# Layer 1's gate and up products by seven half-size products, and sums of squares placed behind later tiles

## The chip, the cores and the metric

The kernel runs on one core of one Trainium2 chip. The metric is the device time of one execution in microseconds, as a median of several runs. The engines of the core are TensorE (PE, with its weight loads PEld), VectorE (DVE), ScalarE (ACT), GpSimd (POOL) and SyncE (SP), which issues most of the transfers.

## What is computed

Two layers of a transformer over 512 latent tokens and 256 context tokens, 1024 features wide, all in float32. Each layer is a token mixer followed by a SwiGLU of 2816 features; each is modulated by a conditioning vector. Layer 0 carries latents and context, layer 1 returns the latents only.

```python
def modulate(x, shift, scale):
    return rms_norm(x) * (1 + scale) + shift

def swiglu(h, w_gate_up, w_down):
    g, u = jnp.split(h @ w_gate_up, 2, axis=-1)
    return (jax.nn.silu(g) * u) @ w_down
...
    for l in range(DEPTH):
        ...
        h_lat = h_lat + g_a * o_lat
        h_lat = h_lat + g_f * swiglu(modulate(h_lat, sh_f, sc_f), ffn_w_gate_up[l], ffn_w_down[l])
        if ctx_out:
            h_ctx = h_ctx + cg_a * o_ctx
            h_ctx = h_ctx + cg_f * swiglu(modulate(h_ctx, csh_f, csc_f), ffn_w_gate_up[l], ffn_w_down[l])
    return rms_norm(h_lat, final_norm)
```

## The kernel before

**Layout.** Features lie on the 128 partitions, tokens along the free axis: eight tiles of 128 x 768 hold the stream (512 latent tokens, `LATS`, then 256 of context, `CTXS`). Every product is made from high and low parts: an operand is cast to a rounded high part on ScalarE (L305, L1193, L1325) and the rest is subtracted on VectorE (L306, L1194, L1326), and each 128-deep step takes three matmuls, high x high, high x low, low x high (L315 to L317 in `mm3`; L1188 to L1190 in `product`; L728 to L730 in `three`).

**Layer 0's SwiGLU (`ffn0`)** already works by seven products. The 768 tokens are two halves of 384 (`TOK1`, `TOK2`), the 1024 input features two halves of four tiles, and gate and up are the two rows of the weight matrix. `combined` makes the operands: "11", "12", "21", "22" are the modulated stream by feature half and token half, and `sums` makes T1 to T4 from their differences, each split into high and low parts. The class `Pair` handles one of the 22 tiles of 128 hidden features, gate and up together. `weights` loads both, splits the gate weights and makes four sums of half weights (S1 to S4, lines L1213 to L1221) with their parts. `head` makes the products with "11" and "21", `body` those with T2, T3 and T1, `tail` those with "22" and T4. Around them ScalarE copies or applies Silu (L1231 to L1246), VectorE adds (L1232, L1242, L1248) and multiplies gate by up (L1250). The first hidden tile, `first_pair`, is made by eight plain products, in the order in which the halves' norms are ready. Pairs are worked in chunks (`CHUNKS0`); after each chunk the down products of its hidden tiles are added to the stream, tile by tile (`add_residual`, L1076).

**Layer 1's SwiGLU (`ffn`)** is plain: for each of 22 hidden tiles, gate and then up, eight input tiles by three matmuls on all 512 latent tokens; for the first two hidden tiles the two halves of 256 tokens (`HALVES`) go one after the other, as their norms become ready. Silu is at L1320, the product at L1324. Four chunks (`CHUNKS`). The input comes from `modulated`: one scale (L382), one ScalarE shift to the high part (L383) and one VectorE low part (L384) for each tile and half.

**Norms and `output`.** `output` makes the last products of a block stream by stream (a stream is a set of token columns), adds them to the residual and adds each tile's squares (ScalarE L347, the add L350 on GpSimd or VectorE). A stream's `Norm.rest` then runs in steps during the next stream's tiles, the first after tile 0: column sums by matmul (L360), square root (L361), reciprocal (L362), a diagonal (L363), a broadcast by matmul (L368), a copy to the tile `nb` (L369), and then `use` for each of the eight tiles. Engines work in order; the order on each is fixed by a scheduler from program order and its own timeline.

**Background.** The modulation vectors are products of `mod_w` with the conditioning. `bg()` advances this work by a step; late in the kernel a step loads a row block into the one tile `rope` and sums it on VectorE (L214). In layer 0's SwiGLU two steps follow each pair (`BG[1]`), and what is left is done in layer 1's `bg(j < 8)` or on demand in `mod()`.

**Buffers.** `b` 24, `st` 12, `p` 8, `wr`, `wh`, `wl` 3 each, `ph` and `pl` 4 each. One pair uses all three of `wh` and `wl`, which the down weights use too.

Of the kernel before, what the change touches and what calls it, by code (L numbers as in the profile page):

```python
# [14 lines left out]
P = 128  # L15
D = 1024
KT = D // P
# [8 lines left out]
CHUNKS = ((0, 6), (6, 6), (12, 5), (17, 5))  # L26
CHUNKS0 = ((0, 4), (4, 4), (8, 4), (12, 4), (16, 3), (19, 3))
# [43 lines left out]
BG = ((0, 0, 0, 0, 0), 2, (0, 0), (0, 0))  # L71
# [28 lines left out]
def hybrid_kernel(ctx: ExitStack, tc, I, out):  # L100
# [1023 lines left out]
    def combined(src, l, comp):  # L1124

        ops = {x: [] for x in ("11", "12", "21", "22", "T1", "T2", "T3", "T4")}
        far, near, room = [], [], {}
# [7 lines left out]
        def both(t, names, tag):  # L1135

            h, lo = split(t, dst=(B(F32R, tag), B(F32R, tag)))
            for i, n in enumerate(names):
                ops[n].append((h[:, i * HT : i * HT + HT], lo[:, i * HT : i * HT + HT]))

        def use(k, r, c, v):
            i, half = k % 4, k // 4
            at = HT * half
            if c is TOK2:
# [4 lines left out]
                if i % 2 == 0:  # L1149
                    room[half] = B(F32R, tag), B(F32R, tag)  # L1150
                x = slice(HT * (i % 2), HT * (i % 2) + HT)
                h, lo = (y[:, x] for y in room[half])
                S.copy(h, far[i][:, at : at + HT])
                V.tensor_tensor(lo, far[i][:, at : at + HT], f(h), op=ALU.subtract)
                ops[name].append((h, lo))
                return
# [3 lines left out]
            if half == 1:  # L1160
                both(near[i], ("11", "21"), "b")

        def sums():

            for i in range(4):
                tag = "st" if i < 2 else "b"
                x, y = B(tag="p"), B(tag="p")
                b11, b21, b12, b22 = near[i][:, TOK1], near[i][:, TOK2], far[i][:, TOK1], far[i][:, TOK2]
                V.tensor_tensor(x[:, TOK1], b12, b11, op=ALU.subtract)
                V.tensor_tensor(x[:, TOK2], b22, x[:, TOK1], op=ALU.subtract)  # L1170
                both(x, ("T1", "T2"), tag)
                V.tensor_tensor(y[:, TOK1], b22, b12, op=ALU.subtract)
                V.tensor_tensor(y[:, TOK2], b21, x[:, TOK2], op=ALU.subtract)
                both(y, ("T3", "T4"), tag)
                yield
# [3 lines left out]
    norm, ops, sums = combined(H, 0, 3)  # L1179
# [12 lines left out]
    def parts(t, h, lo):  # L1192
        S.copy(h, t)  # L1193
        V.tensor_tensor(lo, t, f(h), op=ALU.subtract)  # L1194
        return h, lo

    class Pair:


        def __init__(self, j, tag):  # L1200
            self.j, self.dst = j, [B(F32R, tag) for _ in range(2)]

        def weights(self):
            h = [slice(0, 512), slice(512, 1024)]
            g, u = T("wr", [P, D]), T("wr", [P, D])
            dma(g, I["w_gu"][0, self.j, 0])
            dma(u, I["w_gu"][0, self.j, 1])
# [17 lines left out]
        def head(self):  # L1225
            self.weights()
            self.s, self.t = B(tag="p"), B(tag="p")
            self.z, x = (PG()[:, :HT] for _ in range(2))
            product(self.z, self.g1, ops["11"], True)
            product(x, self.g2, ops["21"], True)  # L1230
            S.copy(self.t[:, TOK2], self.z)  # L1231
            V.tensor_tensor(self.s[:, TOK1], x, self.t[:, TOK2], op=ALU.add)  # L1232
            S.activation(self.s[:, TOK1], self.s[:, TOK1], AF.Silu)

        def body(self):
            self.y = PG()[:, :HT]
            product(self.z, self.s2, ops["T2"])
            S.copy(self.t[:, TOK1], self.z)
            product(self.y, self.s3, ops["T3"], True)
            product(self.z, self.s1, ops["T1"])  # L1240
            S.copy(self.t[:, TOK2], self.z)
            V.tensor_tensor(self.t[:, TOK2], self.y, self.t[:, TOK2], op=ALU.add)  # L1242

        def tail(self):
            product(self.z, self.s4, ops["22"])
            S.activation(self.s[:, TOK2], self.z, AF.Silu)  # L1246
            product(self.y, self.u2, ops["T4"])
            V.tensor_tensor(self.t[:, TOK1], self.y, self.t[:, TOK1], op=ALU.add)  # L1248
            for c in (TOK2, TOK1):
# [3 lines left out]
    def first_pair(tag):  # L1253

        dst, s = [B(F32R, tag) for _ in range(2)], B(tag="p")
        ws = [load_w(I["w_gu"][0, 0, i], KT, P) for i in range(2)]
        for c, a in ((TOK2, ("12", "22")), (TOK1, ("11", "21"))):
            for i, (h, lo) in enumerate(ws):
                o = PG()[:, :HT]
# [11 lines left out]
    def ffn0(new, norm):  # L1271
        tags = ("st", "st", "b", "b")
        for ci, (k0, kc) in enumerate(CHUNKS0):
            hs, last = [], None
            for j in range(k0, k0 + kc):
                if j == 0:
                    hs.append(first_pair(tags[0]))
                    for _ in sums():
                        pass
# [10 lines left out]
                if j > 2:  # L1290
                    bg(BG[1])
            src = lambda m: I["w_dn"][0, m, :, k0 * P : (k0 + kc) * P]
# [3 lines left out]
            if ci < len(CHUNKS0) - 1:  # L1296
                for m in range(KT):
                    t = fetched(m, slice(0, NT))
                    o = banks((LATS, CTXS), PG)
                    mm3(o, ahead.get(m) or load_w(src(m), kc, P), hs)  # L1300
                    for i, (x, c) in enumerate(o):
                        add_residual(m, x, 0, 5, i, c, None, t)
                    dma(home[m], t)
            else:
                new.extend(B() for _ in range(KT))
                old = [fetched(m, slice(0, NT), "b") for m in range(KT)]
                output(src, hs, 0, 5, STREAMS0, norm, BG[3], new, kept_w, lambda m, c: old[m])

    def ffn(l, a, streams, new, norm):
        wide = [c for c, _ in streams] if l == 0 else [LATS]  # L1310
        for ci, (k0, kc) in enumerate(CHUNKS):
            hs = []
            for j in range(k0, k0 + kc):
                cols = [c for c, _ in streams] if j < 2 else wide
                s = B(tag="p")
                dst = [B(F32R, "st") for i in range(2)]
                og = banks(cols, PG)
                mm3(og, load_w(I["w_gu"][l, j, 0], KT, P), a)
                for o, c in og:
                    S.activation(s[:, c], o, AF.Silu)  # L1320
                ou = banks(cols, PG)
                mm3(ou, load_w(I["w_gu"][l, j, 1], KT, P), a)
                for o, c in ou:
                    V.tensor_tensor(s[:, c], s[:, c], o, op=ALU.mult)  # L1324
                    S.copy(dst[0][:, c], s[:, c])  # L1325
                    V.tensor_tensor(dst[1][:, c], s[:, c], f(dst[0][:, c]), op=ALU.subtract)  # L1326
                hs.append(dst)
                bg(j < 8)
            src = lambda m: I["w_dn"][l, m, :, k0 * P : (k0 + kc) * P]
            if ci < len(CHUNKS) - 1:  # L1330
                for m in range(KT):
                    o = banks(wide, PG)
                    mm3(o, load_w(src(m), kc, P), hs)
                    for i, (x, c) in enumerate(o):
                        add_residual(m, x, l, 5, i, c)
            else:
                while new is not None and len(new) < KT:
                    new.append(B())
                output(src, hs, l, 5, streams, norm, BG[3], new, KEEP and new is None)

    new = []
    norm, A = modulated(new, 1, 0, G if E0 else None)
    ffn0(new, norm)
# [89 lines left out]
    norm, a = modulated(H, 1, 3, G if E1 else None)  # L1433
    output(lambda m: I["w_out1"][m], O, 1, 2, STREAMS1, norm, (0, 0))
# [8 lines left out]
    ffn(1, a, STREAMS1, None, Norm(H, finished, G if EF else None))  # L1443
# [104 lines left out]
```

## Time and profile before

| | |
|---|---|
| median of 3 runs | 1643.17 us (1641.32 to 1645.87) |
| profiled execution, its own time | 1641.33 us |
| its span in the profile | 1639.5 us |
| TensorE busy in the span | 1559.8 us, 9190 matmuls |
| VectorE busy | 1092.5 us |
| ScalarE busy | 747.4 us |
| GpSimd busy | 251.9 us |

The span runs from the first to the last instruction. In the rows of the profile, "out<-in" names the tiles, xN the number of instructions, and the bracket what ended the idle time ahead. Times are microseconds from the start of the span; in it layer 0's SwiGLU lies from about 500 to 1016, layer 1's mixer up to 1256, layer 1's SwiGLU from there to 1628.

### The profile page before, as it was taken

Reading aid. Unit: us, or ns where it says so; the run is one execution under the profiler, and the core shown is the slowest. Engines: PE = TensorE matmul, PEld = TensorE weight load, DVE = VectorE, ACT = ScalarE, POOL = GpSimd, SP = SyncE. Lnnn points to the kernel's source line nnn. Section 1 sums busy time; section 2 is a strip of 40 time slices with the busy share of each in tenths; the row PEclk is TensorE's granted clock in tenths of the full one; section 3 lists DMA queues with packets and bytes.
Section 4 is the critical chain, followed back from the end, with each engine's and each line's share of the span. In section 5 each row is a group of like instructions: output and inputs, shape, how many; then the busy total and the mean of one; then the engine's idle time right before and its main releaser. Section 6 shows DMA issues by size and latency. Waiting matters only on the chain.

```text
span 1639.5 us, 24525 instructions
## 1 busy us (share of the span) xinstructions
PE 1559.8 (95%) x9190; PEld 1350.7 (82%) x9190; DVE 1092.5 (67%) x2167; ACT 747.4 (46%) x1470; POOL 251.9 (15%) x184
## 2 busy tenths in 40 slices
PE   4899989999998999999999997999999999999997
PEld 2587867776897999998999996877888888888887
DVE  5994778668578688795858675669867543342435
ACT  6453577677356334242424244457755322222223
POOL 1551734230000000000000003392012000000002
PEclk9899999999999999999999998899999999999998
DMA  9444232002542465646464745121014442232322
GB/s 338 157 151 168 68 120 83 21 8 81 215 180 97 136 209 175 212 141 228 145 209 147 257 142 207 40 89 66 1 63 170 141 130 103 84 109 79 115 76 80
DMA packets 81743, 214.79 MB, mean 131 GB/s; under 512 B 9940, under 2 KB 15576, under 8 KB 81624
## 3 DMA queue, kind: packets, MB, share of 16 engines
q1 hardware_dynamic: 79320, 210.08, 37.9%
q10 hardware_dynamic: 2304, 3.15, 0.5%
q8 instruction: 72, 1.18, 0.3%
q14 instruction: 47, 0.39, 0.1%
HBM read 186.97 MB, written 23.07 MB: 128 GB/s over the span
## 4 chain that ended last, share of the span: by engine, by line
PE 81%; DVE 8%; issue 3%; POOL 3%; ACT 3%; DMA 1%; SPq 0%; POOLq 0%; DVEq 0%; ACTq 0%
PE pss L315 6%; PE pss L317 6%; PE pss L316 6%; PE psd L315 5%; PE psd L316 5%; PE psd L317 5%; PE pso L512 4%; PE pst L315 4%; PE pst L316 4%; PE pst L317 4%; PE pss L1188 3%; PE pss L1189 3%; PE pss L1190 3%; PE pst L459 2%; PE psd L1188 2%
## 5 line engine op out<-in xcount | busy, mean ns | idle before, releaser
L305 ACT CAST wh<-wr 128x1024 fp32r<-128x1024 f32 (+4 forms) x169 | 149.9, 894 | 374.0 <-PE pss L316 89.6
L306 DVE TENSOR_TENSOR wl<-wr,wh 128x1024 fp32r<-128x1024 f32 (+4 forms) x166 | 179.9, 1087 | 125.5 <-ACT wh L305 121.2
L350 POOL TENSOR_TENSOR p<-p,p 128x256 f32<-128x256 f32 (+1 forms) x42 | 45.5, 1084 | 1092.6 <-DMA b<-home 624.9
L316 PE MATMUL pss<-b,wh 128*128 128x256 f32 (+3 forms) x397 | 135.6, 342 | 0.1
L316 PE MATMUL psd<-b,wh 128*128 128x512 f32 (+3 forms) x346 | 121.5, 351 | 0.0
L518 ACT ACTIVATE p<-p,sm 128x512 f32<-128x512 f32 (+3 forms) x144 | 105.1, 730 | 34.8 <-DVE sm L522 32.7
L315 PE MATMUL pss<-b,wh 128*128 128x512 f32 (+3 forms) x341 | 119.1, 353 | 0.7 <-ACT b L383 0.4
L317 PE MATMUL pss<-b,wl 128*128 128x512 f32 (+3 forms) x341 | 119.6, 351 | 0.0
L315 PE MATMUL psd<-b,wh 128*128 128x512 f32 (+3 forms) x306 | 111.6, 365 | 3.3 <-ACT b L418 2.0
L317 PE MATMUL psd<-b,wl 128*128 128x512 f32 (+3 forms) x306 | 109.9, 359 | 0.0
L316 PE MATMUL pst<-b,wh 128*128 128x512 f32 (+2 forms) x277 | 96.2, 347 | 1.8 <-DVE b L384 1.8
L317 PE MATMUL pst<-b,wl 128*128 128x512 f32 (+2 forms) x245 | 86.8, 354 | 1.1 <-DVE wl L306 1.1
L214 DVE CUSTOM_DVE_ANT_0 p<-rope,cond 128x1024 bf16<-128x1024 f32 x64 | 76.9, 1219 | 16.4 <-DMA rope<-in_mod_w_dram 16.4
L315 PE MATMUL pst<-b,wh 128*128 128x512 f32 (+2 forms) x245 | 86.7, 355 | 0.3 <-ACT wh L305 0.3
L316 PEld LDWEIGHTS pss<-b,wh 128*128 128x128 f32 (+1 forms) x397 | 74.4, 187 | 9.2 <-DVE b L1029 0.3
L512 PE MATMUL pso<-ph,b 128*64 128x256 f32 (+1 forms) x384 | 77.4, 360 | 3.2 <-DVE ph L450 3.2
L512 PE MATMUL pso<-pl,b 128*64 128x256 f32 (+1 forms) x384 | 76.7, 359 | 0.2 <-DVE pl L450 0.2
L315 PE MATMUL pss<-st,wh 128*128 128x256 f32 (+2 forms) x215 | 72.9, 339 | 1.1 <-ACT st L1027 0.9
L317 PE MATMUL pss<-st,wl 128*128 128x256 f32 (+2 forms) x215 | 72.4, 337 | 0.1
L315 PEld LDWEIGHTS pss<-b,wh 128*128 128x128 f32 (+1 forms) x341 | 63.5, 187 | 10.5 <-ACT wh L305 0.7
L316 PEld LDWEIGHTS psd<-b,wh 128*128 128x128 f32 (+1 forms) x346 | 65.2, 188 | 7.9 <-issue 0.2
L317 PEld LDWEIGHTS pss<-b,wl 128*128 128x128 f32 (+1 forms) x341 | 63.8, 187 | 8.7
(512 smaller groups left out, 4608.3 us busy)
## 6 DMA issues: line engine op xcount, KB each, us to landing
wr<-in_w_gu_dram SPq DMA_DIRECT2D x88, 512.0 KB, 3.5
rope<-in_mod_w_dram SPq DMA_DIRECT2D x48, 512.0 KB, 3.5
wr<-in_w_out_dram SPq DMA_DIRECT2D x32, 512.0 KB, 3.7
p<-home SPq DMA_DIRECT2D x40, 384.0 KB, 4.4
home<-p SPq DMA_DIRECT2D x40, 384.0 KB, 3.5
wr<-in_w_in_dram SPq DMA_DIRECT2D x21, 512.0 KB, 3.6
wr<-in_w_dn_dram SPq DMA_DIRECT2D x32, 256.0 KB, 3.2
ph<-in_mod_w_dram SPq DMA_DIRECT2D x24, 256.0 KB, 3.5
```

The costliest lines, as they stand in the source:

```text
L214: V.tensor_tensor_reduce(out=T("p", [P, D], mybir.dt.bfloat16), in0=w, in1=cond[:, v, :], op0=ALU.mult, op1=ALU.add, scale=1.0, scalar=0.0 ...
L305: S.copy(h, r)
L306: (G if eng else V).tensor_tensor(lo, r, f(h), op=ALU.subtract)
L315: PE.matmul(o, wh[:, k], mh[:, c], start=first and k == 0, stop=False)
L316: PE.matmul(o, wh[:, k], ml[:, c], start=False, stop=False)
L317: PE.matmul(o, wl[:, k], mh[:, c], start=False, stop=last and k == n - 1)
L350: (eng or V).tensor_tensor(acc[:, :n], acc[:, :n], t[:, :n], op=ALU.add)
L512: ins = PE.matmul(o[64 * i : 64 * i + 64, c], v(kt), t, start=n == 0, stop=n == len(moving[i]) - 1)
L518: S.activation(p[:, c], p[:, c], AF.Exp, bias=nm, scale=-1.0, accum_out=dn)
L1188: PE.matmul(o, wh, xh, start=first and k == 0, stop=False, skip_group_check=not first)
L1189: PE.matmul(o, wh, xl, start=False, stop=False, skip_group_check=not first)
L1190: PE.matmul(o, wl, xh, start=False, stop=k == 3, skip_group_check=not first)
```

## The change

Layer 1's SwiGLU takes the form of layer 0's. `combined` and `Pair` get the layer, the operands and the two token halves as arguments; for layer 1 the halves are `HALVES`, 256 tokens each, and the second half is normed first. As three halves fit in one tile there, T1, T2 and T3 are made in one tile and split at once, and T4 goes into the free third of the tiles of "11" and "21". One function `ffn` serves both layers; layer 1's chunks become six of three or four hidden tiles, all with results in `st`. In layer 1's mixer output the squares are now added on VectorE (`Norm` without an engine). The weights of the last down tile 0 are loaded ahead, as in layer 0.

`output` gets `wait`: the next stream's tiles 0 to wait-1 pass before a step of the earlier stream's `rest` is taken. It is 2 at the end of layer 0's SwiGLU and 1 in both of layer 1's outputs. The background steps after layer 0's pairs become 3 from the twelfth hidden tile on, and layer 1 takes none.

```diff
-CHUNKS = ((0, 6), (6, 6), (12, 5), (17, 5))
-CHUNKS0 = ((0, 4), (4, 4), (8, 4), (12, 4), (16, 3), (19, 3))
+CHUNKS = ((0, 4), (4, 4), (8, 4), (12, 4), (16, 3), (19, 3)), ((0, 3), (3, 3), (6, 4), (10, 4), (14, 4), (18, 4))
...
-BG = ((0, 0, 0, 0, 0), 2, (0, 0), (0, 0))
+BG = ((0, 0, 0, 0, 0), (2, 3), (0, 0), (0, 0))
...
-    def output(src, mov, l, comp, streams, norm, units, dst=None, keep=False, base=None):
+    def output(src, mov, l, comp, streams, norm, units, dst=None, keep=False, base=None, wait=0):
...
                 norm.add(m, c)
-                next(rest, None)
+                if m >= wait:
+                    next(rest, None)
...
-    def combined(src, l, comp):
+    def combined(src, l, comp, c1, c2):
...
             for i in range(4):
                 tag = "st" if i < 2 else "b"
                 x, y = B(tag="p"), B(tag="p")
...
+                V.tensor_tensor(x[:, at1], b12, b11, op=ALU.subtract)
+                V.tensor_tensor(x[:, at2], b22, x[:, at1], op=ALU.subtract)
+                if narrow:
+                    V.tensor_tensor(x[:, at3], b22, b12, op=ALU.subtract)
+                    several(x, ("T1", "T2", "T3"), tag)
+                    V.tensor_tensor(y[:, at1], b21, x[:, at2], op=ALU.subtract)
+                    ops["T4"].append(parts(y[:, at1], *spare[i]))
+                    continue
...
-            for c in (TOK2, TOK1):
+            for c in (self.c2, self.c1) if self.w > NX else (slice(0, 2 * self.w),):
                 V.tensor_tensor(self.s[:, c], self.s[:, c], self.t[:, c], op=ALU.mult)
                 parts(self.s[:, c], *(x[:, c] for x in self.dst))
...
-    def ffn0(new, norm):
-        tags = ("st", "st", "b", "b")
+    def ffn(l, ops, sums, cs, tags, more, down, final):
...
-                    p = Pair(j, tags[j - k0])
+                    p = Pair(l, j, ops, cs, tags[j - k0])
                     p.head()
-                    if j == 1:
+                    if l == 0 and j == 1:
                         bg(2)
                     if last:
                         last.tail()
                     p.body()
                     hs.append(p.dst)
                     last = p
-                if j > 2:
-                    bg(BG[1])
+                bg(more(j))
...
-    def ffn(l, a, streams, new, norm):
-        wide = [c for c, _ in streams] if l == 0 else [LATS]
-        for ci, (k0, kc) in enumerate(CHUNKS):
-            hs = []
-            for j in range(k0, k0 + kc):
-                cols = [c for c, _ in streams] if j < 2 else wide
...
-                mm3(og, load_w(I["w_gu"][l, j, 0], KT, P), a)
...
-                mm3(ou, load_w(I["w_gu"][l, j, 1], KT, P), a)
...
-                bg(j < 8)
...
+    def final0(src, hs):
+        new.extend(B() for _ in range(KT))
+        old = [fetched(m, slice(0, NT), "b") for m in range(KT)]
+        output(src, hs, 0, 5, STREAMS0, norm1, BG[3], new, kept_w, lambda m, c: old[m], 2)
+
+    ffn(0, ops, sums, (TOK1, TOK2), ("st", "st", "b", "b"), lambda j: BG[1][j > 10] if j > 2 else 0, down0, final0)
...
-    norm, a = modulated(H, 1, 3, G if E1 else None)
-    output(lambda m: I["w_out1"][m], O, 1, 2, STREAMS1, norm, (0, 0))
+    norm, ops, sums = combined(H, 1, 3, *HALVES)
+    output(lambda m: I["w_out1"][m], O, 1, 2, ((HALVES[1], 0), (HALVES[0], 0)), norm, (0, 0), wait=1)
...
-    ffn(1, a, STREAMS1, None, Norm(H, finished, G if EF else None))
...
+    def final1(src, hs):
+        keep = lambda src, m: ahead.get(m) or load_w(src(m), len(hs), P, None, "b")
+        output(src, hs, 1, 5, STREAMS1, Norm(H, finished, G if EF else None), (0, 0), None, keep, wait=1)
+
+    ffn(1, ops, sums, HALVES, ("st",) * 4, lambda j: 0, down1, final1)
```

More of the change, by code (lines that the diff above doesn't have):

```diff
@@ L1148, in use @@
                 name, tag = ("12", "22")[half], ("st", "b")[half]
[L1149 to L1155, printed above, removed]
+                h, lo = unit(tag), unit(tag)
+                ops[name].append(parts(far[i][:, at : at + w], h, lo))
                 return
@@ L1160, in use @@
             if half == 1:
-                both(near[i], ("11", "21"), "b")
+                spare.append(several(near[i], ("11", "21"), "b"))
         def sums():
@@ L1244, in tail @@
-        def tail(self):
[L1245 to L1248, printed above, removed]
-            for c in (TOK2, TOK1):
+            self.z, x = (PG()[:, : self.w] for _ in range(2))
+            product(self.z, self.g1, self.ops["11"], True)
+            product(x, self.g2, self.ops["21"], True)
+            S.copy(self.t[:, self.c2], self.z)
@@ L1295, in ffn0 @@
             last.tail()
[L1296 removed]
+            if ci < len(CHUNKS[l]) - 1:
                 for m in range(KT):
[L1298 to L1303, printed above, removed]
[L1304 to L1307 removed]
```

136 lines of the change are left out of this document (66 added, 70 removed).

## The prediction

> **What bounds the kernel now.** I read the page first, then the busy time by stretches, then the order of time around layer 1's second half.
>
> ```profile
> span 1639.5 us, 24525 instructions
> PE 1559.8 (95%) x9190; PEld 1350.7 (82%) x9190; DVE 1092.5 (67%) x2167; ACT 747.4 (46%) x1470; POOL 251.9 (15%) x184
> PE 81%; DVE 8%; issue 3%; POOL 3%; ACT 3%; DMA 1%; SPq 0%; POOLq 0%; DVEq 0%; ACTq 0%
> ```
>
> The third line is the chain of work that ended last: 81% of it is TensorE. The average hides stages, so here are stretches (length; busy PE, PEld, DVE, ACT, POOL; granted clock; DMA share; GB/s):
>
> ```profile
> 598.00:655.00 57.00, 57.00 (x331) 56.65 (x330) 49.17 (x87) 24.32 (x45) 0.00 (x0) 1.00 0.49 166
> 782.00:842.00 60.00, 60.00 (x347) 59.21 (x346) 40.85 (x71) 24.42 (x45) 0.00 (x0) 1.00 0.47 159
> 1256.00:1262.00 6.00, 2.73 (x19) 2.12 (x18) 6.00 (x10) 3.19 (x6) 2.55 (x3) 0.99 0.52 177
> 1262.00:1265.40 3.40, 3.40 (x17) 3.40 (x18) 2.12 (x6) 1.06 (x3) 0.00 (x0) 0.52 0.45 154
> 1265.40:1290.00 24.60, 24.19 (x184) 23.24 (x184) 17.26 (x33) 11.90 (x22) 0.00 (x0) 1.00 0.33 110
> 1290.00:1600.00 310.00, 310.00 (x1362) 254.28 (x1361) 116.98 (x140) 81.69 (x104) 0.00 (x0) 1.00 0.32 103
> ```
>
> The last row is layer 1's SwiGLU: TensorE never stops, VectorE works 117 of 310 us. So time there goes by the number of matmuls and the cost of one. The first two rows are layer 0's SwiGLU, which already has the seven-product form: TensorE full too, VectorE at 49.17/57 = 0.86 and 0.68.
>
> **The gate and up products.** A matmul's busy time contains its latency, so I take start-to-start distances, first and last row of unbroken runs (256, 512 and 384 columns):
>
> ```profile
> 1224.74 0.28 PE L316 MATMUL pss<-b,wh 128*128 128x256 f32 x1
> ...
> 1236.66 0.28 PE L317 MATMUL psd<-st,wl 128*128 128x256 f32 x1
> 1399.86 0.39 PE L315 MATMUL psd<-b,wh 128*128 128x512 f32 x1
> ...
> 1411.88 0.39 PE L317 MATMUL pss<-b,wl 128*128 128x512 f32 x1
> ```
>
> The first run is 101 matmuls, 11.92 us over 100 steps: 0.1192 us. The second is 54, 12.02 over 53: 0.2268 us. Half the columns cost 53%, and this eats most of the seven-for-eight.
> Before, 20 of the 22 feature tiles take 2 x 8 x 3 = 48 matmuls of 512 columns, the first two 96 of 256: 960 x 0.2268 + 192 x 0.1192 = 217.7 + 22.9 = 240.6 us. After, `first_pair` takes 96 of 256 and each of 21 pairs 7 x 4 x 3 = 84 of 256: 1860 x 0.1192 = 221.7 us. **Term A: -18.9 us.** A pair costs 84 x 0.1192 = 10.01 us against 10.89. The down products keep their count; the last chunk only trades a few halves.
> The Trainium skill (TensorE: Matmul & The Clock Gate, Back-to-back issue gap) puts a warm matmul at N/2.4 + 2.5 ns, 109 and 216 ns; by that estimate the pairs would save 21 x (48 x 0.216 - 84 x 0.109) = 25 us. The rows, 10 ns above it at either width, decide.
>
> **VectorE inside the pairs.** Per pair it writes the low part of g (1024 wide), four weight sums and five low parts (512), three half-width adds (256), and one product and one low part (512). Start-to-start again:
>
> ```profile
> 609.41 0.69 DVE L1214 TENSOR_TENSOR ph<-pl,wr 128x512 f32<-128x512 f32 x1
> 610.02 0.68 DVE L1217 TENSOR_TENSOR ph<-wr,wr 128x512 f32<-128x512 f32 x1
> ...
> 627.39 1.22 DVE L1194 TENSOR_TENSOR wl<-wr,wh 128x1024 fp32r<-128x1024 f32 x1
> 628.52 0.55 DVE L1250 TENSOR_TENSOR p<-p,p 128x384 f32<-128x384 f32 x1
> ...
> 1279.28 0.42 DVE L1324 TENSOR_TENSOR p<-p,pst 128x256 f32<-128x256 f32 x1
> 1279.62 1.22 DVE L214 CUSTOM_DVE_ANT_0 p<-rope,cond 128x1024 bf16<-128x1024 f32 x1
> ```
>
> 0.61, 1.13 and 0.34 us. So 1.13 + 11 x 0.61 + 3 x 0.34 = 8.9 us in 10.01 of TensorE: 0.89. Layer 0 carried 0.86 (598 to 655) without a gap, and the down tiles between chunks give VectorE time to run ahead as far as three weight buffers let it. **Term D: +1 us**, bounds 0 and 5. ScalarE (24.3 of 57 in layer 0) has room. The two further chunks add 16 down tiles with their residual adds and loads: hidden under the matmuls of those tiles, VectorE staying under 0.9 over a chunk; DMA at 103 GB/s rises little, as the weights are the same bytes.
>
> **The start of layer 1's SwiGLU.** In order of time, before:
>
> ```profile
> 1259.47 0.47 DVE L1076 SCALAR_TENSOR_TENSOR b<-pss,mod,b 128x256 f32<-128x256 f32 x1
> 1259.61 0.39 PE L316 MATMUL pst<-b,wh 128*128 128x256 f32 x1 [1.77 <-DVE b L384]
> 1261.71 0.90 PE L360 MATMUL psd<-ones,p 128*128 128x1 f32 x4 [1.49 <-POOL p L350]
> 1263.15 0.42 DVE L363 TENSOR_TENSOR p<-ident_r,sm 128x256 f32<-128x256 f32 x1
> 1266.42 0.59 PE L368 MATMUL pss<-p,ones 128*128 128x256 f32 x2
> 1267.53 3.25 DVE L382 SCALAR_TENSOR_TENSOR p<-b,mod,nb 128x256 f32<-128x256 f32 x8 [3.16 <-ACT nb L369]
> 1268.60 0.39 PE L315 MATMUL pss<-b,wh 128*128 128x256 f32 x1 [0.41 <-ACT b L383]
> ```
>
> The second half's norm is late: last residual 1259.47, GpSimd's add of squares, the sum 1261.71, the broadcast only at 1266.42 behind half-clock matmuls (diagonal done 1263.57), first product 1268.60. By the stretches, 1256 to 1290 hold 19 + 17 + 184 = 220 matmuls in 34 us, 10 of them the norm's; 192 of 256 columns and 18 of 512 should take 22.9 + 4.1 = 27.0. So 7 us are lost before: 3.27 and 0.41 idle, some 1.6 of the 3.4 us at clock 0.52, the rest in issues slowed around the waits.
> After, the same 48 products of the first-normed half cover this gap. The adds of squares move from GpSimd to VectorE (0.34 us each, 14 in all) while the modulation sums of mod_w leave this stretch, so VectorE's queue is about as long; the sum of squares no longer ends in a GpSimd add and the broadcast need not wait. I put this first gap at 5 us (2.5 to 7).
> Then a new wait: `sums()` makes T1 to T4 once both halves are modulated, and TensorE reaches the T products soon. From the second half's first scale, VectorE does 8 scales (3.25), four 512 low parts (2.4), the first pair's four ops (1.4), 12 subtractions (4.1), four 768-wide low parts (0.87 each, halfway between 0.61 and 1.13: 3.5), pair 1's three low parts (1.8): 16.5 us. TensorE has a 1.07 us lag (1267.53 to 1268.60), 48 products (5.7) and pair 1's head, 24 (2.9): 9.7. Difference 6.8, and some T2 products overlap while ScalarE's casts add: **7 us** (4 to 9), with the rest of the pair, head 2 and tail 1 queued behind on TensorE. Layer 0 filled this place with mod_wp matmuls; here is none. Half clock after it: 1 us (0 to 3.4), as at 1262 after a shorter gap. Start after: 13 against 7. **Term C: +6 us**, bounds 0 and +11.
> The Trainium skill (TensorE: Matmul & The Clock Gate, The HAM clock gate) has an idle window of about 3.4 us halve the clock. The row's 3.40 us at 0.52 agrees in length, though here two waits of 1.77 and 1.49 us were enough.
>
> **The square sums behind later tiles.** At the end of layer 0:
>
> ```profile
> 1009.22 1.83 PE L360 MATMUL pss<-ones,p 128*128 128x1 f32 x8 [2.82 <-POOL p L350]
> 1011.66 0.69 DVE L363 TENSOR_TENSOR p<-ident_r,sm 128x512 f32<-128x512 f32 x1
> 1016.27 1.02 PE L368 MATMUL pst<-p,ones 128*128 128x512 f32 x2
> ```
>
> TensorE stands 2.82 us before the sum, with the other context tiles queued behind it; then the broadcast, ready at 1012.35, comes 3.9 us late behind them. With wait=2 two tiles more go into the standstill, and fewer lie ahead of the broadcast; GpSimd's chain itself is not shorter. **Term E: -2 us**, bounds -3.9 (broadcast on time) and +1 (the sum itself late behind the added tiles). In layer 1 wait=1 meets no such standstill: nought.
>
> **The background sums.** Ten come after 1230:
>
> ```profile
> L214 DVE CUSTOM_DVE_ANT_0 p<-rope,cond 128x1024 bf16<-128x1024 f32 x10 | 12.2, 1218 | 2.6 <-DMA rope<-in_mod_w_dram 2.6
> ```
>
> They move, with their ten loads on SP's queue, to layer 0's later pairs, where VectorE has 40.85 of 60 us: nought; 12 us if that cover were gone.
>
> **Sum.** -18.9 + 1 + 6 - 2 = -13.9. The profiled execution took 1641.33 us (1639.5 span and 1.8 around it), so 1627.4; on the median of 1643.17, **1629.3**. What counts as changed is 0.3%, 4.9 us: faster is below 1638.2, slower above 1648.1.
>
> **Rivals.**
> *VectorE paces the pairs (slower).* It works in order, each low part waits for a ScalarE cast, and buffers come free only behind TensorE. Decisive from 10.7 us a pair (13.9 + 1 over 21 pairs), where VectorE gets only 0.83 of the time to work. At 11.2 us it costs 25 instead of 1: 1653. For: 0.89 is above anything seen. Against: 0.86 with no gap at all. Chance 0.09.
> *A long start (no change).* If each of the two first pairs waits for its sums and low parts in series, VectorE's 3.25 + 2.4 + 1.4 + 10.5 + 2 x 8.9 = 35 us plus some 8 of ScalarE between stand against 26 of TensorE: 17 lost, 5 before and 2 at half clock, C = +17: 1640. Chance 0.10.
> *The start is hidden (faster still).* The order lets VectorE make pair 1's weights early and the first gap closes: C = 0, E = -3.9, 1621. Chance 0.08.
> *Weight loads bind (slower, by far).* Per tile 84 loads replace 48:
>
> ```profile
> L316 PEld LDWEIGHTS pss<-b,wh 128*128 128x128 f32 x56 | 10.5, 188 | 0.0
> ```
>
> At 188 ns one after another a pair takes 15.8 us, +121 in all: 1751. The same rows stand in the 0.1192 run, so loads overlap. Chance 0.01. The Trainium skill (Perfetto Trace Analysis, Identifying the Most-Contended Engine) would judge TensorE's headroom by this busy share, 56.65 of 57 in layer 0: by that rule no room is left and the change loses; the 0.1192 run contradicts it.
>
> **How the numbers follow.** The forecast has 0.72, of which 0.02 lies within 0.3%. Faster 0.70 + 0.08 = 0.78, same 0.10 + 0.02 = 0.12, slower 0.09 + 0.01 = 0.10. The range runs from the hidden start, 1620, to just above the long one, 1642, and leaves out the two slower rivals and the edges.
>
> **What would show it.** Right: 256-column runs at 0.119 to 0.121 in layer 1's SwiGLU, pairs near 10.0 us, one TensorE gap of 4 to 9 us ending on a VectorE low part of the T operands, half clock after it, no L214 after 1230. Wrong: TensorE idle in every pair before L1188-type products with VectorE or ScalarE as releaser (pairs over 10.7 us); gaps at both first pairs; the sum of squares at the end of layer 0 waiting as long as now; TensorE gaps in layer 0's pairs 11 to 21.

## The result, and the profile after

The changed kernel takes 1644.58 us (median of 14 runs, 1641.27 to 1651.29), the kernel before 1644.59 in the same sessions (14 runs): ratio 1.0002, interval 0.9991 to 1.0014. No change; the forecast was 1629.3, with 1642 as its upper end. The profiled execution after took 1644.78 us. First the span, the busy time of the engines and the chain of work that ended last, from the page after:

```profile
span 1643.0 us, 26444 instructions
...
PE 1550.8 (94%) x9874; PEld 1371.9 (84%) x9874; DVE 1226.6 (75%) x2462; ACT 820.2 (50%) x1672; POOL 234.6 (14%) x170
...
PE 73%; DVE 11%; DMA 7%; issue 4%; ACT 3%; POOL 1%; SPq 0%; POOLq 0%; DVEq 0%; ACTq 0%
```

TensorE is busy for 9 us less, but its part of the chain fell from 81% to 73% and that of DMA rose from 1% to 7%. New waits have eaten the gain, and some of them end on a transfer.

To place them, three moments of the kernel before in its order of time: the first matmul of `w_out1`, the last of layer 1's SwiGLU, and the norm's sum that ends the kernel.

```profile
1207.89 0.39 PE L315 MATMUL pst<-st,wh 128*128 128x256 f32 x1
...
1627.89 0.28 PE L317 MATMUL psd<-st,b 128*128 128x256 f32 x1
...
1630.11 0.68 PE L360 MATMUL pss<-ones,p 128*128 128x1 f32 x4 [1.94 <-POOL p L350]
```

The same moments after, with two more ahead of the last two rows, the first and the last of an unbroken run of 216 products:

```profile
1217.47 0.39 PE L314 MATMUL pst<-st,wh 128*128 128x256 f32 x1
...
1331.10 0.28 PE L1204 MATMUL pss<-b,wh 128*128 128x256 f32 x1
...
1357.04 0.28 PE L1206 MATMUL psd<-b,wl 128*128 128x256 f32 x1
...
1628.99 0.28 PE L316 MATMUL pss<-st,b 128*128 128x256 f32 x1
...
1633.27 1.01 PE L359 MATMUL pss<-ones,p 128*128 128x1 f32 x4 [4.00 <-POOL p L349]
```

Before `w_out1` starts, in code whose only edits of substance are a rate of background steps and the argument `wait`, 9.6 us are lost (1217.47 against 1207.89). From there to the last matmul of SwiGLU 8.5 us are won (411.5 against 420.0). Behind it 2.1 us are lost (4.28 to the sum, against 2.22). Together +3.2 of the span's +3.5.

Layer 1's SwiGLU after, by stretches (length; busy PE, PEld, DVE, ACT, POOL; granted clock; DMA share; GB/s):

```profile
1265.00:1311.00 46.00, 36.72 (x247) 34.54 (x246) 36.89 (x76) 25.59 (x55) 0.00 (x0) 0.85 0.17 52
1311.00:1603.00 292.00, 291.31 (x2030) 270.19 (x2030) 224.49 (x366) 140.12 (x269) 0.00 (x0) 1.00 0.32 102
```

From 1311 on TensorE stands for 0.7 us of 292 and VectorE works 0.77 of the time: the pairs run as forecast. The start holds 247 matmuls in 46 us; at the forecast's 0.1192 us they take 29.4, so 16.6 us are lost there, against 7 before and a forecast of 13. These are the four longest waits behind it:

```profile
1271.18 1.02 PE L359 MATMUL psd<-ones,p 128*128 128x1 f32 x4 [1.98 <-DVE p L349]
...
1273.21 1.22 PE L367 MATMUL pss<-p,ones 128*128 128x256 f32 x2 [1.01 <-DVE p L362]
...
1280.96 0.38 PE L728 MATMUL psd<-b,wh 128*128 128x256 f32 x1 [1.93 <-DVE b L339]
...
1294.08 0.43 PE L1205 MATMUL pss<-b,wh 128*128 128x256 f32 x1 [1.92 <-DVE b L339]
```

All end on VectorE: the add of squares, the diagonal, and low parts of the modulated tokens (L339 is the low part in `split`; at 1294 it belongs to a T operand). TensorE stands for 9.3 us of the 46. The other 7 us lie in matmuls that came at half the pace behind both gaps, at half the granted clock:

```profile
1273.00:1277.00 4.00, 3.79 (x16) 3.62 (x16) 1.98 (x6) 2.51 (x5) 0.00 (x0) 0.50 0.49 168
1297.00:1301.00 4.00, 4.00 (x20) 4.00 (x20) 2.24 (x5) 1.19 (x3) 0.00 (x0) 0.50 0.37 98
```

### The profile page after: what moved, and what is told of

It is laid out like the page before. It is cut to its first block, busy times and chain, and to the rows that moved or that the text cites. A ratio compares the mean times of both kernels' runs of the same rounds, so it can differ in the third digit from the quotient of the medians.

```text
span 1643.0 us, 26444 instructions
## 1 busy us (share of the span) xinstructions
PE 1550.8 (94%) x9874; PEld 1371.9 (84%) x9874; DVE 1226.6 (75%) x2462; ACT 820.2 (50%) x1672; POOL 234.6 (14%) x170
## 4 chain that ended last, share of the span: by engine, by line
PE 73%; DVE 11%; DMA 7%; issue 4%; ACT 3%; POOL 1%; SPq 0%; POOLq 0%; DVEq 0%; ACTq 0%
PE pso L511 4%; PE pss L1204 4%; PE pss L1206 4%; PE pss L1205 4%; PE pss L314 4%; PE pss L315 4%; PE pss L316 4%; PE psd L314 3%; PE psd L315 3%; PE psd L316 3%; PE pst L1204 3%; PE pst L1206 3%; PE pst L1205 3%; PE pst L314 3%; PE pst L316 3%
## 5 line engine op out<-in xcount | busy, mean ns | idle before, releaser
L304 ACT CAST wh<-wr 128x1024 fp32r<-128x1024 f32 (+2 forms) x144 | 109.7, 774 | 205.6 <-PE pst L315 49.3
L305 DVE TENSOR_TENSOR wl<-wr,wh 128x1024 fp32r<-128x1024 f32 (+2 forms) x141 | 131.4, 937 | 78.3 <-ACT wh L304 77.8
L1205 PE MATMUL pss<-b,wh 128*128 128x384 f32 (+1 forms) x346 | 107.5, 311 | 1.9 <-DVE b L339 1.9
L1204 PE MATMUL pss<-b,wh 128*128 128x384 f32 (+1 forms) x346 | 108.2, 313 | 0.6 <-ACT b L338 0.6
L1206 PE MATMUL pss<-b,wl 128*128 128x384 f32 (+1 forms) x346 | 106.9, 311 | 0.0
L213 DVE CUSTOM_DVE_ANT_0 p<-rope,cond 128x1024 bf16<-128x1024 f32 x64 | 77.0, 1222 | 32.7 <-DMA rope<-in_mod_w_dram 32.5
L315 PE MATMUL psd<-b,wh 128*128 128x512 f32 (+3 forms) x242 | 83.0, 343 | 0.0
L314 PE MATMUL psd<-b,wh 128*128 128x512 f32 (+3 forms) x210 | 75.4, 359 | 3.3 <-ACT b L417 2.1
L315 PE MATMUL pss<-b,wh 128*128 128x256 f32 (+3 forms) x229 | 73.0, 320 | 2.8 <-DVE b L1192 2.7
L1191 ACT CAST wh<-ph 128x512 fp32r<-128x512 f32 x84 | 48.4, 619 | 50.7 <-PE psd L1205 16.2
L1205 PEld LDWEIGHTS pss<-b,wh 128*128 128x128 f32 x346 | 65.7, 190 | 2.3 <-DVE b L339 2.1
L1204 PEld LDWEIGHTS pss<-b,wh 128*128 128x128 f32 x346 | 66.0, 191 | 1.5 <-ACT b L338 0.8
L1206 PE MATMUL psd<-b,wl 128*128 128x384 f32 (+1 forms) x212 | 66.3, 314 | 0.6 <-DVE wl L1192 0.6
L1204 PE MATMUL psd<-b,wh 128*128 128x384 f32 (+1 forms) x212 | 66.6, 314 | 0.0
L1205 PE MATMUL psd<-b,wh 128*128 128x384 f32 (+1 forms) x212 | 66.4, 313 | 0.0
```

What stands on the lines that cost most here:

```text
L213: V.tensor_tensor_reduce(out=T("p", [P, D], mybir.dt.bfloat16), in0=w, in1=cond[:, v, :], op0=ALU.mult, op1=ALU.add, scale=1.0, scalar=0.0 ...
L304: S.copy(h, r)
L305: (G if eng else V).tensor_tensor(lo, r, f(h), op=ALU.subtract)
L314: PE.matmul(o, wh[:, k], mh[:, c], start=first and k == 0, stop=False)
L315: PE.matmul(o, wh[:, k], ml[:, c], start=False, stop=False)
L1204: PE.matmul(o, wh, xh, start=first and k == 0, stop=False, skip_group_check=not first)
```

## Where layer 0 lost its time

The fourth of layer 0's six chunks holds pairs 12 to 15. TensorE's waits in and behind it, and one at layer 0's end, after:

```profile
818.31 0.45 PE L1206 MATMUL pst<-b,wl 128*128 128x384 f32 x1 [1.39 <-DVE wl L1192]
...
837.41 0.58 PE L315 MATMUL pss<-b,wh 128*128 128x256 f32 x1 [2.73 <-DVE b L1192]
...
999.50 0.50 PE L314 MATMUL pss<-st,st 128*128 128x512 f32 x1 [1.67 <-ACT p L1258]
```

In and behind the chunk VectorE is late, so look at what it does in these 58 us: the row of stretches, after, and then all that it waited for there (us in total, times, longest):

```profile
783.00:841.00 58.00, 53.88 (x303) 52.91 (x302) 43.57 (x75) 21.83 (x42) 0.00 (x0) 0.97 0.48 153
```

```profile
DVE p L213 <- DMA rope<-in_mod_w_dram: 13.2, 9, 3.2
DVE wl L1192 <- ACT wh L1191: 1.1, 1, 1.1
```

The same two views before (of the waits, the three longest):

```profile
783.00:841.00 58.00, 58.00 (x335) 57.21 (x335) 38.85 (x68) 23.12 (x45) 0.00 (x0) 1.00 0.48 164
```

```profile
DVE wl L306 <- ACT wh L305: 7.5, 3, 5.7
DVE p L1242 <- ACT p L1241: 4.1, 2, 2.9
DVE p L214 <- DMA rope<-in_mod_w_dram: 3.6, 4, 1.8
```

VectorE is busy for only 0.75 of the time after. Work and waits together fill a stretch on any engine (43.57 + 14.3 after, 38.85 + 19.0 before, of 58), so the sum says little; what counts is what the waits end on and what stands behind them. After, 13.2 us are waits for the loads of `mod_w`, ahead of sums that nobody needs soon, and since VectorE works in order the low parts of the pair's weights wait behind them. Before, it waited longer, but mostly for ScalarE and only 3.6 us for these loads, and TensorE never stood for it.

What sets the pace of the steps is the one buffer. Sum and load of a step follow each other through the tile `rope0`. The first and the last of the twelve sums of this stretch in the order of time, after, and the loads by issue:

```profile
783.90 1.22 DVE L213 CUSTOM_DVE_ANT_0 p<-rope,cond 128x1024 bf16<-128x1024 f32 x1
...
839.82 1.22 DVE L213 CUSTOM_DVE_ANT_0 p<-rope,cond 128x1024 bf16<-128x1024 f32 x1 [0.86 <-DMA rope<-in_mod_w_dram]
```

```profile
rope<-in_mod_w_dram SPq DMA_DIRECT2D x11, 512.0 KB, 3.5
```

Twelve sums start over 55.9 us: 5.1 us a step, of which 1.2 are the sum and 3.5 the load from issue to landing. Two steps a pair take 10.2 us; three take 15.3. And a pair of layer 0, from an unbroken run of 300 matmuls before:

```profile
777.79 0.34 PE L1188 MATMUL psd<-b,wh 128*128 128x384 f32 x1
...
829.72 0.33 PE L1190 MATMUL psd<-b,wl 128*128 128x384 f32 x1
```

is 84 matmuls at 51.93/299 = 0.174, 14.6 us. Two steps fit beside it, three don't. The Trainium skill (DMA: Bandwidth & Descriptors, Anatomy of one DMA — SWDGE (gpsimd) path) fits a transfer that GpSimd issues at about 2.0 us + bytes/436e3; by that estimate 512 KB take 3.2 us. The row's 3.5, issued by SyncE, is near it; in the run below whose loads GpSimd issues they took 3.8.

At layer 0's end a second price is paid. The sums of the last chunk reach to 987.8 us, and the table of layer 1's rotation, which takes the same buffer, and the loads queued behind it on SyncE come late (the table is issued at 987.84 against 974.57 before, the first reload of the stream behind it at 1001.69 against 989.70); from the first tiles of the last down phase to the first norm's sum it is 26.1 us (996.3 to 1022.4) against 21.2 before (988.0 to 1009.2).

The theory: (1) layer 0 loses some 10 us to the third step a pair, by its load; (2) layer 1's start loses about 4 us more than forecast, to the sums of tokens; (3) the end loses 2. Rivals: the start alone ate the gain; VectorE's work, not the loads, cost layer 0; the waits put into `output` cost.

## The experiments

Each line of the table gives the ratio to the kernel before and its interval; the changed kernel stands at 1.0002.

| kernel | median us | ratio | interval |
|---|---|---|---|
| after, ten steps' loads and sums left out | 1639.90 | 0.9972 | 0.9961 to 0.9983 |
| before, three steps a pair from the twelfth | 1651.34 | 1.0044 | 1.0031 to 1.0058 |
| after, ten steps in the down phases | 1633.94 | 0.9941 | 0.9927 to 0.9955 |
| after, second pair by plain products | 1638.33 | 0.9959 | 0.9947 to 0.9972 |
| after, `wait` at nought | 1647.97 | 1.0020 | 1.0011 to 1.0029 |
| after, adds of squares on GpSimd | 1645.85 | 1.0005 | 0.9996 to 1.0014 |
| after, loads of `mod_w` issued by GpSimd | 1644.16 | 0.9996 | 0.9987 to 1.0006 |
| after, steps that load nothing | 1636.81 | 0.9955 | 0.9942 to 0.9967 |
| after, down phases and plain products | 1629.75 | 0.9904 | 0.9889 to 0.9919 |
| the same, last adds on VectorE | 1628.70 | 0.9907 | 0.9893 to 0.9922 |

### The last ten steps left out

```
+            drop = l == 1 and (comp == 5 or comp == 3 and m > 5)
+            if not drop:
                 w = late[0]()
                 dma(w, I["mod_w"][at])
...
+                if drop:
+                    V.memset(MOD[l, comp, v][:, m : m + 1], 1.0)
```

> The changed kernel with the loads and sums of the last ten steps of mod_w left out: the eight columns of layer 1's component 5 and the last two of component 3 are set to the constant 1 in their place, at the same places in the order. Theory (the ten steps that moved into layer 0's pairs cost about 9 us there, by the one buffer that they share and by SyncE's queue, and a little more at layer 1's start): 9 to 11 us less than the changed kernel, about 1634, layer 1's mixer at the same offset as in the kernel before within 2 us. Rival 1 (the layer 0 lag comes from the waits put into output, or from something else that moved; the start of layer 1's SwiGLU alone eats the gain): at most 3 us less, 1641 to 1645. Rival 2 (what layer 0 loses is given back later by slack in the mixer): the mixer starts earlier, the end within 3 us of the changed kernel's.

Measured: 4.9 us less than the changed kernel, half of what the theory said and more than rival 1 allows. My edit was the wrong one: the ten steps left out are the last in the order, while the third step a pair begins at the twelfth pair and draws the others forward. VectorE's sums and their idle time before them, over the whole kernel:

```profile
L218 DVE CUSTOM_DVE_ANT_0 p<-rope,cond 128x1024 bf16<-128x1024 f32 x54 | 64.8, 1223 | 25.0 <-DMA rope<-in_mod_w_dram 24.7
```

Ten sums fewer, but 24.7 us of waiting for loads are left, of 32.5 after and 16.4 before. Pairs 12 to 15 still had their three steps, and still lost time.

### That one part in the kernel before

```
-                    bg(BG[1])
+                    bg(BG[1] + (j > 10))
```

> The kernel before, with this one part of the change: three steps of mod_w a pair in place of two from the twelfth pair of layer 0 on, so that layer 1's pairs find none left. Theory: the ten steps cost layer 0 about 9 us and give VectorE in layer 1's old pairs nothing that the end depends on, so 7 to 10 us slower than the kernel before, 1651 to 1655. Rival 1 (they are free in layer 0): within 2 us of the kernel before. Rival 2 (they cost there, but their absence from layer 1's old start gives a part back): 2 to 6 us slower.

Measured: 7.2 us slower (5.1 to 9.5), as the theory had it. The pattern of pairs 12 to 15 comes back whole in a kernel that has nothing else of the change:

```profile
784.00:842.00 58.00, 53.62 (x300) 52.65 (x299) 43.20 (x75) 21.85 (x42) 0.00 (x0) 0.97 0.47 152
```

```profile
DVE p L214 <- DMA rope<-in_mod_w_dram: 13.3, 9, 2.5
DVE wl L1194 <- ACT wh L1193: 1.4, 2, 1.0
```

Again 13.3 us of waits for these loads, and TensorE at 53.62. So the loss isn't layer 1's products, the chunks or the waits in `output`.

### The ten steps in the down phases

```
-BG = ((0, 0, 0, 0, 0), (2, 3), (0, 0), (0, 0))
+BG = ((0, 0, 0, 0, 0), (2, 2), (0, 0), (0, 0))
...
                     down(m, lambda: ahead.get(m) or load_w(src(m), kc, P), hs)
+                    bg(l == 0 and m in (2, 5))
```

> The changed kernel with two steps a pair all through layer 0, and the other ten put into its first five down phases, one behind each third and each sixth tile, where VectorE and SyncE's queue have more time. Theory: layer 0 ends within 2 us of the kernel before's offsets, 7 to 11 us less than the changed kernel, 1634 to 1638. Rival 1 (a step costs the same wherever in layer 0 it stands, since its load holds up SyncE's queue): within 2 us of the changed kernel. Rival 2 (the start of layer 1's SwiGLU alone eats the gain): at most 3 us less.

Measured: 10 us less than the changed kernel and 9.7 less than the kernel before (7.4 to 12.0), the same work in the same layer at another place. The loads are all there, at a DMA share of 0.51 in the stretch, so it isn't the transfers as such that cost. TensorE stands no more in the stretch, and `w_out1` starts at 1206.01, 1.9 us ahead of the kernel before:

```profile
783.00:841.00 58.00, 58.00 (x335) 57.21 (x335) 39.75 (x69) 22.90 (x45) 0.00 (x0) 1.00 0.51 173
```

```profile
1206.01 0.39 PE L314 MATMUL pst<-st,wh 128*128 128x256 f32 x1
```

### The loads or the sums?

```
             w = late[0]()
-            dma(w, I["mod_w"][at])
+            G.dma_start(w, I["mod_w"][at])
```

> The changed kernel with the loads of mod_w that stand in layer 0 from its mixer's end on issued by GpSimd in place of SyncE, so that no load behind them in SyncE's queue waits for the one buffer; the sums stay where they are. If SyncE's queue carries layer 0's loss: 6 to 9 us faster than the changed kernel, 1636 to 1639. If the sums' own waits for the loads, in VectorE's order, carry it: within 2 us. Theory holds both for part: 3 to 7 us faster.

```
-            w = late[0]()
-            dma(w, I["mod_w"][at])
+            w = cond[:, 0, :]
```

> The changed kernel with three steps a pair as it has them, but the steps from the end of layer 0's mixer on load nothing: each sums over a row of the resident conditioning tile in place of a row of mod_w, so that VectorE's work is the same and the one buffer and its loads are gone. Theory (three trips of some 4.8 us through the one buffer don't fit into a pair of 13.4 us, and what stands behind them, on VectorE and in SyncE's queue, is late): layer 0's loss goes, 8 to 11 us less than the changed kernel, 1634 to 1637. Rival (VectorE's own work in a pair, 1.2 us a sum, is what layer 0 lost): within 2 us of the changed kernel.

Without loads, at the same rate and with the same sums: 7.7 us less than the changed kernel; 1636.81 lies just inside the theory's 1634 to 1637, and the 7.7 just short of its 8 (my text has the pair at 13.4 us there, which is wrong; it is 14.6). The stretch without loads:

```profile
783.00:841.00 58.00, 57.81 (x331) 56.62 (x330) 46.50 (x81) 23.91 (x45) 0.00 (x0) 1.00 0.31 98
```

VectorE does more than after, 46.50 against 43.57, which is 0.80 of the time, and TensorE hardly stands. So the work of the sums fits; their loads did not. That falsifies the rival of VectorE's work.

Loads issued by GpSimd changed nothing in the sum (0.9996). But in the stretch itself TensorE was full:

```profile
783.00:841.00 58.00, 58.00 (x335) 57.48 (x334) 44.98 (x78) 23.97 (x47) 5.28 (x10) 1.00 0.45 144
```

```profile
DVE p L213 <- DMA rope<-in_mod_w_dram: 7.8, 7, 2.4
DVE wl L1192 <- ACT wh L1191: 3.4, 3, 1.6
```

although the steps there lie no closer (787.50 to 848.79, 5.6 us each). So three trips that are longer than a pair need not hold TensorE up; it matters what waits behind the loads.

That execution was already 4.1 us late at 226 us (the same matmul of L711 starts at 229.67 against 225.57), ahead of GpSimd's first load at 289 us, so its times compare only from a common point on. From the first product of layer 0's second chunk to `w_out1` it takes 619.5 us; the changed kernel takes 622.9, the run without loads 613.0, the one with ten steps in the down phases 612.5, the kernel before 614.0. By these traces the run without loads wins back all that layer 0 lost, and GpSimd's queue about 3 of the 10 us: in the fourth chunk, from its first product to that of the fifth, 93.4 us in place of 98.0 (91.9 before), and about 1 us is lost again behind it. The medians bear out no more than 0.4 us. How the 10 us divide between VectorE's waits and the loads behind `mod_w` in SyncE's queue stays open. That queue stood in front of `mod_w` loads for 40.0 of these 58 us in the changed kernel (26.4 until the load before had landed, 13.6 until its sum was done), but for 32.4 in the kernel before too.

### The second pair by plain products

```
-                if j == 0:
-                    hs.append(first_pair(l, ops, cs, tags[0]))
-                    sums()
+                if j < 1 + l:
+                    hs.append(first_pair(l, j, ops, cs, tags[j]))
+                    if j == 0:
+                        sums()
```

> The changed kernel with the second pair of layer 1 also by eight plain products (12 more matmuls of 128x256, 1.4 us), so that the sums of the tokens and their splits have a second pair of some 11 us to run beside. Theory: of the 17 us that TensorE loses at the start of layer 1's SwiGLU, 7 to 10 go, and the sum is 5 to 8 us less than the changed kernel, 1637 to 1640; the 9 us of layer 0 stay. Rival 1 (the loss at the start lies on squares, the norm's sums and the first loads, not on the sums of tokens): 0 to 2 us slower than the changed kernel. Rival 2 (the start alone eats the gain): 10 us and more less.

Measured: 7 us less than the changed kernel, although 1.4 us of products were added. The same 46 us of the start now hold 311 matmuls, 37.1 us at 0.1192, so 8.9 us are lost in place of 16.6, and no wait for a T operand is left:

```profile
1265.00:1311.00 46.00, 41.80 (x311) 39.97 (x310) 35.34 (x75) 25.85 (x55) 0.00 (x0) 0.93 0.21 61
```

Rival 2 (the start alone ate the gain) is out: of the 9.6 us by which the start's loss had grown 7.7 went, and the kernel still stood 9 us above the forecast.

### Squares on GpSimd, and `wait` at nought

```
-        return Norm(src, use, None, (0, 4, 1, 5, 2, 6, 3, 7)), ops, sums
+        return Norm(src, use, G if l else None, (0, 4, 1, 5, 2, 6, 3, 7)), ops, sums
```

> The changed kernel with the adds of layer 1's squares at w_out1 back on GpSimd, where the kernel before has them. Theory: the second stream's sum, which waited 1.98 us for an add that stood behind the second pair's weight sums on VectorE, comes 1 to 2 us sooner, and TensorE loses that much less at the start: 1 to 2 us faster than the changed kernel, 1642.5 to 1643.5. Rival (what ends the start's waits is the sums of tokens and their splits, so that the sooner norm only waits longer there): within 1 us of the changed kernel.

Measured: 1.0005, nothing gained; the theory's 1 to 2 us fell, the rival held. The sum of squares waited 0.83 us in place of 1.98, but the next step waited longer in VectorE's queue:

```profile
1270.65 0.61 PE L359 MATMUL psd<-ones,p 128*128 128x1 f32 x4 [0.83 <-POOL p L349]
...
1274.54 1.22 PE L367 MATMUL pss<-p,ones 128*128 128x256 f32 x2 [3.28 <-DVE p L362]
...
1295.97 0.39 PE L1205 MATMUL pss<-b,wh 128*128 128x256 f32 x1 [2.16 <-DVE b L339]
```

By this the start goes by VectorE's queue as a whole, which in the changed kernel is busy without a break from 1277 to 1297 us, not by one add in it.

```
-        output(src, hs, 0, 5, STREAMS0, norm1, BG[3], new, kept_w, lambda m, c: old[m], 2)
+        output(src, hs, 0, 5, STREAMS0, norm1, BG[3], new, kept_w, lambda m, c: old[m])
...
-    output(lambda m: I["w_out1"][m], O, 1, 2, ((HALVES[1], 0), (HALVES[0], 0)), norm, (0, 0), wait=1)
+    output(lambda m: I["w_out1"][m], O, 1, 2, ((HALVES[1], 0), (HALVES[0], 0)), norm, (0, 0))
...
-        output(src, hs, 1, 5, STREAMS1, Norm(H, finished, G if EF else None), (0, 0), None, keep, wait=1)
+        output(src, hs, 1, 5, STREAMS1, Norm(H, finished, G if EF else None), (0, 0), None, keep)
```

> The changed kernel with the added argument at nought in all three places, so that the norm's steps follow the first tile of the next stream again, as before the change. Theory: the wait of 2 at the end of layer 0 earned 2 to 4 us there, the two waits of 1 earn about 1 us at the end of w_out1 and cost about 2 us at the kernel's end: the sum 1 to 4 us slower than the changed kernel, 1646 to 1649. Rival (the waits cost, and are what the forecast missed): 3 us and more faster than the changed kernel, 1641 or less.

Measured: 1.0020, 3 us slower than the changed kernel, as the theory had it. From the first product of layer 0's last chunk to the start of `w_out1` it took 273.55 us (945.80 to 1219.35) against 272.00 (945.47 to 1217.47), so some 1.5 us of it are layer 0's end. One part of the theory fell: the wait of 1 doesn't cost 2 us at the kernel's end, where the last sum waits as long without it:

```profile
1219.35 0.39 PE L314 MATMUL pst<-st,wh 128*128 128x256 f32 x1
...
1636.45 1.01 PE L359 MATMUL pss<-ones,p 128*128 128x1 f32 x4 [3.93 <-POOL p L349]
```

### Two edits together, and the end

> Two edits of the runs before together: the ten steps in layer 0's down phases, and layer 1's second pair by eight plain products. Theory (two losses at two places, one behind the other, so their prices add): 10.7 and 6.3 us together, 16 to 18 us less than the changed kernel, 1627 to 1629. Rival (the second loss is partly the first's: later loads at the start because layer 0 ends late): 11 to 14 us less, 1631 to 1634.

Measured: 0.9904, 15.8 us less than the kernel before (13.3 to 18.2), 16 less than the changed kernel; both edits are those shown above. The two prices add within the noise: 10 and 7 apart, 16 together. The rival's 11 to 14 touches only the lower edge of the interval. This version beats both kernels. On it, the end's chain of adds was tried on VectorE:

```
-E0, E1, EF = 1, 1, 1
+E0, E1, EF = 1, 1, 0
```

> The version of the run before with the ten steps in the down phases and the second pair by plain products, and with the adds of the last norm's squares on VectorE in place of GpSimd. Theory (the end's sum waited 4.1 us for a chain of GpSimd's adds of 0.74 us, since the last down phase has tiles of 1.4 us in place of 1.8): 1 to 2.5 us less than that version, 1627 to 1628.5. Rival (the adds then stand behind the scaling of the first stream on VectorE, and wait as long): within 1 us of it.

Measured: 0.9907, the same within the interval. The rival held: the sum waits as long, now for VectorE, where the adds stand between the scalings of the first half:

```profile
1617.25 1.01 PE L359 MATMUL pst<-ones,p 128*128 128x1 f32 x4 [4.48 <-DVE p L349]
```

What holds the last sum is not GpSimd's pace in the adds alone. In that trace ScalarE has the last square done at 1614.1 us, and VectorE the last add of squares at 1617.2:

```profile
1614.39 0.95 DVE L349 TENSOR_TENSOR p<-p,p 128x256 f32<-128x256 f32 x2
1615.26 0.88 DVE L1426 SCALAR_TENSOR_TENSOR p<-b,final_norm,nb 128x256 f32<-128x256 f32 x2
1616.05 0.42 DVE L349 TENSOR_TENSOR p<-p,p 128x256 f32<-128x256 f32 x1
1616.38 0.48 DVE L1426 SCALAR_TENSOR_TENSOR p<-b,final_norm,nb 128x256 f32<-128x256 f32 x1
1616.78 0.42 DVE L349 TENSOR_TENSOR p<-p,p 128x256 f32<-128x256 f32 x1
```

An order with the adds ahead of these scalings was not tried.

## Why the prediction was wrong, by its own steps

**Term A (-18.9) and term D (+1) held.** The run of 216 products has 0.1207 us from start to start (25.94 over 215), where the forecast had 0.1192 and rival one needed 10.7 us a pair, 0.127. From `w_out1` to the last matmul 8.5 us were won, with 16.6 lost at the start against 7: the products and VectorE's part in them gave about 18 us, against 17.9 forecast. VectorE was busy for 22.86 of the run's 25.94 us, 0.88 where 0.89 was forecast (0.77 with the down phases), and TensorE stands for only 0.7 us in 292. The pairs and loads behaved as argued; the rival of the weight loads is out too.

**The background sums ("nought; 12 us if that cover were gone") failed, and this is the cause of the miss.** They cost 10 us (the third experiment), 7.2 in the kernel before. The step took VectorE's busy time, 40.85 of 60 us, as the cover, and never priced a step's trip through its one buffer: 5.1 us, of which the sum is 1.2. Two trips take 10.2 us beside a pair of 14.6, three 15.3, and what stands behind the loads, in VectorE's order and in SyncE's queue, then comes late; without the loads and with the same sums layer 0 lost nothing. How much of the 10 us goes by which of the two is not shown. The Trainium skill (Perfetto Trace Analysis, Identifying the Most-Contended Engine) takes VectorE's occupancy as a fair measure of how near its limit it is; here TensorE waited for VectorE in a stretch where it was busy for 0.75 of the time, and stood for no more than 0.2 us in the same stretch without loads at 0.80, or in the run of 216 products at 0.88. The measurement decides. That the 12 us named as the price without cover had the right size is luck: it was ten sums of 1.2 us, and what was paid were loads.

**Term C (+6) was small by 4, and its parts came out otherwise.** 16.6 us were lost in place of 13. The wait for a low part of the T operands is there, but its longest piece is 1.92 us where 7 were forecast, and TensorE stood for 9.3 us in all; half clock, forecast at 1 us behind the second gap, took most of the other 7. That the sum is nearer than its parts is luck. VectorE needed 22.8 us from the second half's first scale to the last low part of T1 to T3 (1275.78 to 1298.57), not 16.5: the forecast's list left out T4's subtractions and low parts and most of the second pair's weight work, which stand between. The sum of squares waited 1.98 us for an add behind the second pair's weight sums, which the forecast's count of VectorE's queue ahead of the norm left out too; taking that add away gained nothing. A second pair of cover took 7 us off.

**Term E (-2) held for layer 0**: 1.5 us by the run with `wait` at nought, and 1.9 between the kernel before (269.2 us from the last chunk's first product to `w_out1`) and the one with ten steps in the down phases (267.3). And the "nought" for layer 1 was a gain of about 1 (0.8 us from `w_out1`'s start to the first down tile, against the run with `wait` at nought). Not foreseen were 2 us at the kernel's end, where the last half's tiles take 1.4 us in place of 1.8 (4 feature tiles in place of 5, 12 products of 0.119 in place of 15) and the chain of squares behind them does not get shorter.

So 10 us went in layer 0, 4 at the start and 2 at the end. That is 2 more than the -13.9, within what single executions differ: the two profiled ones are 3.5 us apart where the medians are equal. With the first alone put right the kernel took 1633.9 us, inside the forecast's range. "TensorE gaps in layer 0's pairs 11 to 21" stood among the signs of a wrong forecast, but no rival carried a price for it.

## What to carry to other kernels

Before work is moved beside other work, price its trip and not only its busy time: load, use and release of the buffer, times the number of trips, against the stretch that should hide them. Then ask what stands behind the trip, on the engine that uses the buffer and in the queue that issues the load. Idle time of an engine that works in order is not room as long as it isn't known what its waits end on and who waits behind them. A step that nobody needs soon belongs where the engine is ahead of the bound, as here in the down phases, not where it barely keeps up.

## What the runs showed of the hardware that was not expected

A chain of load and sum through one buffer ran at 5.1 us a step, where the load landed in 3.5 and the sum took 1.2; issued from GpSimd's queue the load took 3.8 us and a step 5.6, and still VectorE's waits for loads in the stretch fell from 13.2 to 7.8 us, with no gain in the median. Behind waits of 1.98 and 1.01 us, and again behind one of 1.92, matmuls of 256 columns came 0.213 us apart in place of 0.119 (up to about 1277.2 and 1301.1 us, the granted clock at 0.50). An add of 128x256 takes GpSimd 0.74 us and VectorE 0.34 from start to start, but to move a chain of them from one to the other changed the time in neither place where it was tried.
